# First stage of a hybrid decoder layer: statistics by group of three blocks, loads and bias tables in a new order

## The chip, the cores and the metric

The kernel runs on one core of a Trainium2 chip. A core has five engines with queues of their own: TensorE (PE in the profile, its weight loads PEld), VectorE (DVE), ScalarE (ACT), GpSimd (POOL) and SyncE (SP), which here issues nearly all transfers. The metric is the device time of one execution in microseconds (us), as the median of several; lower is better.

## The reference

One decoder layer over 16 learned meta rows and 1024 tokens, width 1024, all in float32:

```python
h = concatenate([meta, x])
a = rmsnorm(h, ln_mix_pre)                 # h * rsqrt(mean(h*h) + eps) * gain
dq, dk, dv, hq, hf, hi, hg = split(a @ w_in)
y_diff = diff_attention(dq, dk, dv, ...)   # 4 heads, two softmaxes each, T5 bias table by distance
y_hgrn = hgrn2(hq, hf, hi, hg, ...)        # 4 heads of a gated recurrence
h = h + rmsnorm(concatenate([y_diff, y_hgrn]) @ w_out, ln_mix_post)
h = h + rmsnorm(conv_ffn(rmsnorm(h, ln_ffn_pre)), ln_ffn_post)
out = h[16:]
```

The change touches the first lines only: the RMS norm ahead of the input projection, the projections dq, dk and dv of head 0, and the small tables that attention and recurrence need (the relative-position bias, the lower bounds of the gate, the lambda of the differential attention).

## The kernel before

**Precision by halves.** A float32 product is made from three matmuls: each operand is a rounded part (hi) and the remainder (lo), and hi·hi, hi·lo and lo·hi are summed in PSUM. So each operand costs a cast (mostly on ScalarE) and a subtraction (on VectorE or GpSimd): `ahi` and `alo` are the halves of the activations, `wh_` and `wl_` those of the weights from the raw load `wr_` (for dv: `w` from `wv`).

**Blocks and groups.** The rows are nine blocks: block 0 is the 16 meta rows, blocks 1 to 8 are 128 tokens each. Three blocks make a group: 272 columns in group 0, 384 in groups 1 and 2. A projection of one head is 128 output columns; for one group it takes 8 slices of the inner dimension by 3 products, 24 matmuls, each with the weights stationary.

**The first stage**, everything that the change touches, works on a transposed copy of the input (`xt`, tiles `xr`), which can go into the matmuls at once, and on the plain rows (`x`, `xm` for the meta rows), of which only the sums of squares are wanted:
- `x_stat(i)`: for one block ScalarE squares and sums its rows (an activation and the reading of its accumulator), takes the reciprocal root by a logarithm and an exponential, and scales an identity matrix by it (tile `dg`).
- `x_spread(g)` (L297): TensorE multiplies ones with the three `dg` of a group, which spreads the factors over all partitions in a PSUM tile `prs`.
- `x_norm`, `x_hi`, `x_lo`: for each of 8 slices VectorE multiplies `xr` by gain and factor, ScalarE casts to `ahi`, VectorE or GpSimd subtracts to `alo`.
- `Kinds.mm` (L843) issues a projection's matmuls (tiles `pi_dq`, `pi_dk`, `pi_dv`), and `out()` evacuates a finished one: q and k by ScalarE and VectorE in halves (`q`, `k`, `kl`), v by ScalarE into `vt`, which `flush()` later has TensorE transpose (`pn_va`) and ScalarE copy to `avn`.
- `smalls` and `lam_terms` compute the gate's bounds (`lg`, `lmx`, `lb` and others) and lambda (`lv`, `le`, `nlam`) from small loads. `bias_tables` loads a one-hot matrix (`ohr`) and the table (`tb`), casts both (`oh`, `tbb`), and for each head multiplies them (L354, tile `pb`), copies the product to `rb`, subtracts a column, fills a third of it and stores it to `rsc` in DRAM, from where attention reads it.

After the stage the heads follow: `proj_step` (L248, L250, L252) issues the matmuls of all later projections, hf, hq, hi and hg of head 0 first, with attention woven between, and `load_split` (L165) loads their weights.

**What sets the order.** TensorE's instructions run as the program issues them, everywhere. For VectorE, ScalarE and GpSimd a planner sets the order by its own costs, but while `state["ordered"]` is true (the first stage up to the marked line) each instruction issued through `V`, `A` or `G` keeps its place in program order on its engine. SP's transfers, issued through `SY`, are left to the planner throughout. A tile waits for the buffer of its tag: the tag `m` has five PSUM banks in this stage (`prs`, `pn`, `pb` and the projections of group 1 use it), the tag `ip` three; `rb` has one buffer, `ss` and `dg` three, and the plain rows of blocks 1 to 8 go through four slots. The weight halves `wh` and `wl` have four buffers, which dq and dk of head 0 fill and hf and hq take next.

## Time and profile before

| | us |
|---|---|
| median of 3 runs (1293.88 to 1297.57) | 1294.78 |
| profiled execution | 1295.81 |
| its span | 1293.8 |
| TensorE busy in the span (97%) | 1256.9 |
| VectorE (70%), ScalarE (53%), GpSimd (40%) | 910.2, 692.1, 511.8 |

The span runs from the first to the last instruction of the profiled execution; the 2.0 us between span and time lie around it. Busy time is the sum of an engine's instructions; TensorE's matmuls overlap one another, so a busy TensorE need not be at its peak, and the granted clock (1.00 is full) is shown beside it. In the rows below, `out<-in` names the tiles by the program's names, `xN` is a count of merged instructions, and the bracket at the end gives the idle time of the engine ahead of the row and what ended it. A timeline row begins with its start and its length in us; L58 is the helper through which the engines other than TensorE are issued, so those rows are told apart by their tiles.

### The profile page before, as it was taken

How to read it: one execution, taken by the hardware profiler on the slowest of the kernel's cores; microseconds unless marked ns; L12 is line 12 of the kernel's file. 1: busy time of each engine (PE TensorE's matmuls, PEld its weight loads, DVE VectorE, ACT ScalarE, POOL GpSimd, SP SyncE). 2: the span in 40 equal slices, each digit the busy share in tenths (PEclk: the TensorE clock that was granted, in tenths of full speed). 3: DMA queues.
4: the chain of work that ended last, by engine and by line, in shares of the span. 5: the costliest groups of instructions: out<-in, count | busy, mean ns of one | idle time of the engine just before them, and what ended most of it. 6: DMA issues, size and time to landing. Idle time of an engine off the chain costs nothing.

```text
span 1293.8 us, 25973 instructions
## 1 busy us (share of the span) xinstructions
PE 1256.9 (97%) x10108; PEld 1174.3 (91%) x10108; DVE 910.2 (70%) x1496; ACT 692.1 (53%) x1653; POOL 511.8 (40%) x394
## 2 busy tenths in 40 slices
PE   5699999999999999999999999999999999999997
PEld 5599999999999999778899999999999998878886
DVE  3557455654656465558798888888888967797586
ACT  6665457545754665346775445445444454554454
POOL 5232233342314220345056776776776731010121
PEclk9899999999999999999999999999999999999999
DMA  8236356545565531778512222222223237965363
GB/s 323 80 101 114 91 107 131 107 89 112 118 129 88 114 91 52 231 242 283 200 31 93 90 66 91 90 66 91 82 67 99 66 107 248 353 196 171 90 212 122
DMA packets 117710, 169.28 MB, mean 131 GB/s; under 512 B 10370, under 2 KB 58050, under 8 KB 117588
## 3 DMA queue, kind: packets, MB, share of 16 engines
q1 hardware_dynamic: 94356, 156.10, 37.2%
q0 software_dynamic: 23232, 11.54, 7.6%
q8 instruction: 79, 1.29, 0.4%
q14 instruction: 43, 0.35, 0.1%
HBM read 138.50 MB, written 52.17 MB: 147 GB/s over the span
## 4 chain that ended last, share of the span: by engine, by line
PE 45%; DVE 5%; ACT 2%; issue 1%; DMA 0%; SPq 0%; DVEq 0%; ACTq 0%
PE pd L1562 5%; PE pd L1563 4%; PE pd L1561 4%; PE pb L1388 4%; PE pb L1387 4%; PE pb L1389 4%; PE pc L1388 3%; PE pc L1387 3%; PE pc L1389 3%; PE pa L1388 3%; PE pa L1387 3%; PE pa L1389 3%; DVE xh L58 1%; DVE t L58 1%; ACT a L58 1%
## 5 line engine op out<-in xcount | busy, mean ns | idle before, releaser
L1388 PE MATMUL pb<-t,uh 128*128 128x258 f32 x504 | 141.0, 280 | 0.8 <-DVE t L58 0.8
L1387 PE MATMUL pb<-t,uh 128*128 128x258 f32 x504 | 140.5, 279 | 0.8 <-DVE u L58 0.8
L1389 PE MATMUL pb<-t,ul 128*128 128x258 f32 x504 | 140.2, 278 | 0.0
L1562 PE MATMUL pd<-wl,gh 128*128 128x512 f32 (+1 forms) x312 | 121.0, 388 | 1.5 <-DVE wl L58 1.5
L1561 PE MATMUL pd<-wh,gh 128*128 128x512 f32 (+1 forms) x312 | 120.7, 387 | 0.5 <-DVE x L58 0.5
L1563 PE MATMUL pd<-wh,gl 128*128 128x512 f32 (+1 forms) x312 | 120.8, 387 | 0.0
L58 DVE SCALAR_TENSOR_TENSOR c<-uu,cwt,c 128x514 f32<-128x514 f32 (+1 forms) x88 | 107.0, 1215 | 0.0
L58 DVE SCALAR_TENSOR_TENSOR c<-ug,cwt,c 128x514 f32<-128x514 f32 (+1 forms) x88 | 101.6, 1155 | 0.0
L1388 PEld LDWEIGHTS pb<-t,uh 128*128 128x128 f32 x504 | 94.8, 188 | 1.0 <-DVE t L58 1.0
L1387 PEld LDWEIGHTS pb<-t,uh 128*128 128x128 f32 x504 | 94.8, 188 | 1.0 <-DVE u L58 1.0
L58 ACT ACTIVATE c<-c 128x514 f32<-128x514 f32 (+1 forms) x44 | 27.9, 634 | 125.5 <-DVE c L58 125.5
L1389 PEld LDWEIGHTS pb<-t,ul 128*128 128x128 f32 x504 | 94.8, 188 | 0.0
L1388 PE MATMUL pc<-t,uh 128*128 128x258 f32 (+1 forms) x336 | 94.3, 281 | 0.0
L1387 PE MATMUL pc<-t,uh 128*128 128x258 f32 (+1 forms) x336 | 94.2, 280 | 0.0
L1388 PE MATMUL pa<-t,uh 128*128 128x258 f32 (+1 forms) x336 | 94.0, 280 | 0.0
L1389 PE MATMUL pc<-t,ul 128*128 128x258 f32 (+1 forms) x336 | 93.9, 279 | 0.0
L1387 PE MATMUL pa<-t,uh 128*128 128x258 f32 (+1 forms) x336 | 93.7, 279 | 0.0
L1389 PE MATMUL pa<-t,ul 128*128 128x258 f32 (+1 forms) x336 | 93.5, 278 | 0.0
L58 POOL TENSOR_TENSOR ul<-ws,uh 128x512 fp32r<-128x512 f32 x42 | 69.2, 1647 | 59.7 <-ACT uh L58 59.7
L58 POOL TENSOR_TENSOR ws<-ra,ra 128x512 f32<-128x512 f32 x42 | 67.4, 1604 | 61.5 <-DVE c L58 31.3
L58 POOL TENSOR_TENSOR c<-c,c 128x514 f32<-128x514 f32 (+1 forms) x44 | 69.0, 1567 | 54.9 <-ACT c L58 49.9
L58 DVE TENSOR_TENSOR ul<-ra,uh 128x512 fp32r<-128x512 f32 x43 | 41.2, 959 | 46.9 <-POOL ul L58 46.9
(384 smaller groups left out, 4187.5 us busy)
## 6 DMA issues: line engine op xcount, KB each, us to landing
ra<-in_wup_dram SPq DMA_DIRECT2D x88, 256.0 KB, 2.6
mp<-msc SPq DMA_DIRECT2D x23, 512.0 KB, 5.6
tsc<-in_wdown_dram SPq DMA_DIRECT2D x44, 256.0 KB, 5.1
wi<-tsc SPq DMA_DIRECT2D x44, 256.0 KB, 3.1
gi<-gsc SPq DMA_DIRECT2D x33, 256.0 KB, 4.6
wi<-in_wdown_dram SPq DMA_DIRECT2D x33, 256.0 KB, 5.3
gsc<-c SPq DMA_DIRECT2D x22, 257.0 KB, 2.1
tsc<-in_wdown_dram POOLq DMA_DIRECT2D x22, 256.0 KB, 7.1
```

The costliest lines, as they stand in the source:

```text
L58: ins = call(*args, **kw)
L1387: T.matmul(pt, hi[:, s], th[:, k], start=(first and k == 0), stop=False, skip_group_check=True)
L1388: T.matmul(pt, hi[:, s], tl[:, k], start=False, stop=False, skip_group_check=True)
L1389: T.matmul(pt, lo[:, s], th[:, k], start=False, stop=(k == 3), skip_group_check=True)
L1561: T.matmul(py, gh[:, s], wh, start=(k == 0 and pr not in (3, 7)), stop=False, skip_group_check=True)
L1562: T.matmul(py, gh[:, s], wl, start=False, stop=False, skip_group_check=True)
L1563: T.matmul(py, gl[:, s], wh, start=False, stop=(k == NH - 1), skip_group_check=True)
```

## The change

Statistics are taken for a whole group: the three sums of squares go into the columns of one tile, with one logarithm and one exponential for the three, and the diagonals are made on VectorE. The meta rows are squared and summed on VectorE, the other blocks on ScalarE. Block 5 gets its own place beside the meta rows, in the buffer that later holds the transposed rows of group 2. The loads are issued in a new order, with the one-hot matrix and the bias table ahead of the second transposed group; the casts of both come ahead of the statistics of group 1. Hi and lo products of the first half of dq and dk are issued together. The statistics of group 2 come ahead of the evacuation of group 0; the tables of heads 0 and 1, then the spread and the norm of group 2, come before the last products of group 1; `alo` of group 2 is made on GpSimd in place of VectorE; dv and dk of group 2 are issued in the ordered part, and the tables of heads 2 and 3 between the products of dq and dk. `smalls` and `lam_terms` come after all this in the program, and `issue_after` puts them behind the last norm on VectorE and the last cast on ScalarE.

```diff
-    def x_stat(i):
-        r = rows(i)
-        ss = zp.tile([P, 1], F32, tag="ss", name=f"ss{i}", bufs=3)
-        A.activation(x_rows[i][:r], x_rows[i][:r], AF.Square, accum_out=ss[:r])
-        rstd_of(ss[:r], ss[:r], D)
-        dg = zp.tile([P, P], F32, tag="dg", name=f"dg{i}", bufs=3)
-        A.mul(dg[:r, :r], ident[:r, :r], ss[:r])
-        return dg
+    def x_stats(g, on_vector=()):
+        blks = range(*GROUPS[g])
+        ss = zp.tile([P, 3], F32, tag="ss", name=f"ss{g}", bufs=3)
+        if g == 0:
+            V.memset(ss, 1.0)
+        for c, i in sorted(enumerate(blks), key=lambda b: b[1] == 0):
+            r = rows(i)
+            if i in on_vector:
+                V.tensor_tensor(x_rows[i][:r], x_rows[i][:r], x_rows[i][:r], op=ALU.mult)
+                V.reduce_sum(ss[:r, c:c + 1], x_rows[i][:r], axis=AX.X)
+            else:
+                A.activation(x_rows[i][:r], x_rows[i][:r], AF.Square, accum_out=ss[:r, c:c + 1])
+        rstd_of(ss, ss, D)
+        res = {}
+        for c, i in enumerate(blks):
+            r = rows(i)
+            res[i] = zp.tile([P, P], F32, tag="dg", name=f"dg{i}", bufs=3)
+            V.tensor_scalar(res[i][:r, :r], ident[:r, :r], ss[:r, c:c + 1], None, ALU.mult)
+        return res
...
-    def bias_tables():
+    def bias_loads():
...
+        return oh, raw, tb
+
+    def bias_casts(oh, raw, tb):
         tbb = zp.tile([64, HEADS, P], F32R, tag="tbb", name="tbb", bufs=1)
         A.copy(oh, raw)
...
+        return tbb, oh
-        for h in range(HEADS):
...
+    def bias_table(h, tbb, oh):
+        pt = ps_m(f"pb{h}")
+        T.matmul(pt[:, :384], tbb[:, h], oh, start=True, stop=True)
+        rb = zp.tile([P, 512], F32, tag=f"wv{h}", name=f"rb{h}", bufs=1)[:, :384] if h < 2 else zp.tile([P, 384], F32, tag="rb", name=f"rb{h}", bufs=1)
+        V.tensor_copy(rb, pt[:, :384])
+        V.tensor_scalar(rb[:, :256], rb[:, :256], rb[:, 0:1], None, ALU.subtract)
+        V.memset(rb[:, 256:], NEG)
+        SY.dma_start(rsc[h].rearrange("(p c) -> p c", p=P), rb)
...
-    x_rows = {0: zp.tile([P, KD * 3 * P], F32, tag="xr2", name="xm", bufs=1)[:, :D]}
-    for i in range(1, NBLK):
-        x_rows[i] = slots[(i - 1) % 4]
+    spare = zp.tile([P, KD * 3 * P], F32, tag="xr2", name="xm", bufs=1)
+    x_rows = {0: spare[:, :D], 5: spare[:, D:2 * D]}
+    for n, i in enumerate((1, 2, 3, 4, 6, 7, 8)):
+        x_rows[i] = slots[n % 4]
...
     for i in (1, 2, 0):
         load_x(i)
-    SY.dma_start(gcol, gpre)
     open_xt(0)
     open_xt(1)
-    for c in range(2):
-        load_xt(0, 4 * c, 4 * c + 4)
-        for j in range(2):
-            load_raw(j, c)
-    for i in (3, 4):
+    load_raw(0, 0)
+    load_xt(0, 0, 4)
+    SY.dma_start(gcol, gpre)
+    load_raw(1, 0)
+    load_xt(0, 4, 8)
+    for j, c in ((0, 1), (1, 1), (2, 0), (2, 1)):
+        load_raw(j, c)
+    for i in (3, 4, 5):
         load_x(i)
-    for c in range(2):
-        load_raw(2, c)
+    bias = bias_loads()
     for c in range(2):
         load_xt(1, 4 * c, 4 * c + 4)
...
-    stats = {i: x_stat(i) for i in (1, 2, 0)}
+    stats = x_stats(0, (0,))
     spread = {0: x_spread(0, stats)}
-    for i in (5, 6):
+    for i in (6, 7):
         load_x(i)
-    open_xt(2)
-    for c in range(2):
-        load_xt(2, 4 * c, 4 * c + 4)
     w_hi(0, 0, G)
+    w_lo(0, 0, G)
     w_hi(1, 0, G)
-    w_lo(0, 0, G)
     w_lo(1, 0, G)
     for k in range(KD):
         x_norm(0, k, spread[0])
         x_hi(0, k)
+        if k == 3:
+            w_hi(0, 1, A)
         if k == 5:
-            for j in range(2):
-                w_hi(j, 1, A)
+            w_hi(1, 1, A)
...
-    for i in (3, 4, 5):
-        stats[i] = x_stat(i)
-    for i in (7, 8):
-        load_x(i)
+    for m in range(2):
+        G.memset(az[m], 0.0)
+    tbb = bias_casts(*bias)
+    stats = x_stats(1)
+    open_xt(2)
+    for c in range(2):
+        load_xt(2, 4 * c, 4 * c + 4)
+    load_x(8)
     dq, dk, dv = first = [Kinds(j, 0, ps_in) for j in range(3)]
-    for half in range(2):
-        for k in range(4 * half, 4 * half + 4):
-            for kd in (dq, dk):
-                kd.mm(k, 0, ahi)
-    for half in range(2):
+    for k in range(4):
         for kd in (dq, dk):
-            kd.part(half, 1, ahi)
+            kd.mm(k, 0, ahi)
+            kd.mm(k, 1, ahi)
+    for k in range(4, KD):
+        for kd in (dq, dk):
+            kd.mm(k, 0, ahi)
+    for kd in (dq, dk):
+        kd.part(1, 1, ahi)
...
+    stats = x_stats(2)
     for kd in first:
         kd.out()
-    for m in range(2):
-        G.memset(az[m], 0.0)
-    for i in (6, 7, 8):
-        stats[i] = x_stat(i)
     second = [Kinds(j, 1, ps_m) for j in range(3)]
     for k in range(KD):
         for kd in second:
             kd.mm(k, 0, ahi)
             kd.mm(k, 1, ahi)
+    for h in range(2):
+        bias_table(h, *tbb)
+    spread[2] = x_spread(2, stats)
+    for k in range(KD):
+        last_norm = x_norm(2, k, spread[2])
+        last_hi = x_hi(2, k)
+        x_lo(2, k, G)
     flush()
-    smalls()
-    lam_terms()
-    tables = bias_tables()
-    next(tables)
-    for j, kd in enumerate(second):
+    for kd in second:
         for half in range(2):
             kd.part(half, 0, alo)
-        if j == 0:
-            spread[2] = x_spread(2, stats)
+        kd.out()
+    dq, dk, dv = [Kinds(j, 2, ps_in) for j in range(3)]
     for k in range(KD):
-        x_norm(2, k, spread[2])
-        x_hi(2, k)
-    for kd in second:
+        for kd in (dq, dk):
+            kd.mm(k, 0, ahi)
+            kd.mm(k, 1, ahi)
+    for h in range(2, HEADS):
+        bias_table(h, *tbb)
+    flush()
+    for kd in (dq, dk):
+        for half in range(2):
+            kd.part(half, 0, alo)
         kd.out()
-    for k in range(KD):
-        last_lo = x_lo(2, k, V)
-    dq = Kinds(0, 2, ps_in)
     for w, a in ((0, ahi), (1, ahi), (0, alo)):
         for half in range(2):
-            dq.part(half, w, a)
-    dq.out()
-    flush()
+            dv.part(half, w, a)
+    dv.out()
     state["ordered"] = False
-
-    def head0():
-        for j, (m, name, evac) in enumerate(tiles):
-            if j:
-                yield from proj_group(2, parts[j], name, evac)
-
-    interleave(head0(), [tables], 2600)
+    with tc.issue_after(last_norm.ins), tc.issue_after(last_hi.ins):
+        smalls()
+        lam_terms()
```

More of the change, by code (lines that the diff above doesn't have):

```diff
@@ L301, in x_norm @@
     def x_norm(g, k, pt):
-        V.scalar_tensor_tensor(xr[g][:, k], xr[g][:, k], gcol[:, k:k + 1], pt, ALU.mult, ALU.mult)
+        return V.scalar_tensor_tensor(xr[g][:, k], xr[g][:, k], gcol[:, k:k + 1], pt, ALU.mult, ALU.mult)
     def x_hi(g, k):
-        A.copy(ahi[:, k, cols(g)], xr[g][:, k])
+        return A.copy(ahi[:, k, cols(g)], xr[g][:, k])
     def x_lo(g, k, eng):
@@ L351, in bias_tables @@
         V.tensor_tensor(tbb[32:], tbr[32:].to_broadcast([32, HEADS, P]), tbb[32:].bitcast(F32), op=ALU.subtract)
-        for h in range(HEADS):
-            pt = ps_m(f"pb{h}")
-            T.matmul(pt[:, :384], tbb[:, h], oh, start=True, stop=True)
-            rb = zp.tile([P, 384], F32, tag="rb", name=f"rb{h}", bufs=1)
-            V.tensor_copy(rb, pt[:, :384])
-            V.tensor_scalar(rb[:, :256], rb[:, :256], rb[:, 0:1], None, ALU.subtract)
-            G.memset(rb[:, 256:], NEG)
-            SY.dma_start(rsc[h].rearrange("(p c) -> p c", p=P), rb)
-            yield
+        return tbb, oh
[7 more added lines that the diff above has]
+        SY.dma_start(rsc[h].rearrange("(p c) -> p c", p=P), rb)
     def to_nat(dst, srcT, b0, b1, name):
```

## The prediction

> **What bounds the kernel now.** I read the busy time of two stretches first (columns: stretch, length, then busy time and instructions of PE, PEld, DVE, ACT and POOL, granted clock, DMA share, GB/s), then PE's own waits in the first 80 us, longest first.
>
> ```profile
> 0.00:75.00 75.00, 51.93 (x248) 45.89 (x249) 32.21 (x75) 45.00 (x105) 28.16 (x38) 0.91 0.54 192
> 75.00:1293.80 1218.80, 1205.01 (x9862) 1128.37 (x9861) 877.95 (x1421) 647.10 (x1549) 483.66 (x356) 1.00 0.45 127
> ```
>
> ```profile
> PE prs L297 <- ACT dg L58: 10.6, 1, 10.6
> PE pb L354 <- DVE tbb L58: 7.6, 1, 7.6
> ...
> PE pi_dq L843 <- DVE alo L58: 1.9, 1, 1.9
> ```
>
> TensorE stands idle for 23.1 of the first 75 us (75.00 - 51.93) and for 13.8 of the other 1218.8. From 75 us on only the amount of matmul work counts, and the change leaves that alone; what it can win or lose lies before the first matmul of the HGRN projections (hf). The timeline says where that is, and what stands ahead of the 7.6 us wait:
>
> ```profile
> 37.53 0.27 PE L368 MATMUL pn_va<-ident,vt 128*128 128x128 f32 x1
> ...
> 42.16 0.16 DVE L58 TENSOR_TENSOR lmx<-lg 128x4 f32<-128x4 f32 x1 [5.11 <-ACT lg L58]
> ...
> 44.77 0.68 DVE L58 TENSOR_TENSOR tbb<-tb,tbb 32x512 fp32r<-32x512 f32 x1
> ...
> 74.58 0.29 PE L248 MATMUL pi_hf<-ahi,wh_hf 128*128 128x272 f32 x1
> ```
>
> The table matmul pb needs only tbb, but VectorE, in program order, reaches tbb after the small terms, and these stood 5.11 us for lg, an activation queued on ScalarE behind the squares of group 2. Idling also costs clock (the column before DMA's share):
>
> ```profile
> 46.00:48.00 2.00, 2.00 (x7) 1.82 (x7) 0.93 (x2) 0.00 (x0) 0.20 (x1) 0.50 0.00 0
> ...
> 56.00:58.00 2.00, 0.68 (x4) 0.36 (x3) 1.94 (x4) 1.93 (x5) 0.00 (x0) 1.00 0.00 0
> 58.00:60.00 2.00, 1.32 (x3) 0.66 (x3) 1.99 (x5) 0.13 (x1) 0.00 (x0) 0.88 0.00 0
> 60.00:62.00 2.00, 2.00 (x6) 1.25 (x5) 1.85 (x4) 0.62 (x1) 0.50 (x1) 0.50 0.00 0
> ...
> 66.00:68.00 2.00, 2.00 (x12) 1.85 (x10) 0.15 (x1) 0.62 (x1) 0.14 (x1) 0.91 0.37 125
> ```
>
> After the 7.6 us wait the matmuls run at half clock, and again from 60 to past 66, after the 1.9 us wait for alo.
>
> **Part 1: up to the first spread.**
>
> ```profile
> DMA to landing us min/median/max: 4.5/4.5/4.5
> ```
>
> ```profile
> 1.64 0.43 SPq L281 DMA_DIRECT2D xm<-in_meta_dram  x1
> ...
> 8.38 1.04 ACT L58 ACTIVATE xm<-xm 16x1024 f32<-16x1024 f32 x1
> ...
> 10.55 1.73 PE L297 MATMUL prs<-dg,ones 16*128 16x16 f32 x6 [10.55 <-ACT dg L58]
> ...
> 12.32 3.36 DVE L58 SCALAR_TENSOR_TENSOR xr<-xr,gcol,prs 128x272 f32<-128x272 f32 x8 [12.32 <-PE prs L297]
> ...
> 13.41 0.57 PE L843 MATMUL pi_dq<-ahi,wh_dq 128*128 128x272 f32 x1 [1.13 <-ACT ahi L58]
> 15.59 2.90 DVE L58 TENSOR_TENSOR alo<-xr,ahi 128x272 fp32r<-128x272 f32 x8
> 15.91 3.72 POOL L58 TENSOR_TENSOR wl_dq<-wr_dq,wh_dq 128x512 fp32r<-128x512 f32 x1 [2.77 <-ACT wh_dq L58]
> 18.16 1.11 PE L843 MATMUL pi_dq<-ahi,wl_dq 128*128 128x272 f32 x4
> 19.60 1.27 POOL L58 TENSOR_TENSOR wl_dk<-wr_dk,wh_dk 128x512 fp32r<-128x512 f32 x1
> 22.00 1.16 PE L843 MATMUL pi_dv<-ahi,w 128*128 128x272 f32 x8
> ```
>
> Before, ScalarE does squares, logarithm, exponential and diagonal for one block after another and ends with the meta block. Now the two big squares come first and the meta rows go to VectorE: a multiply and a sum, 1024 columns each. A 272-column subtraction on VectorE goes at 0.36 us (2.90 for eight), 1.3 ns a column with its overhead, so each of the two costs 1.1 to 1.36; I take 1.2. The meta rows land at 6.1 (1.64 + 4.5), the sum is there at 8.5, logarithm and exponential take it to 9.1, the first of three short diagonals to 9.6. The first spread thus starts at **9.6 in place of 10.55**. Bounds: 8.5, were VectorE free of cost, and 10.5, were each of its two passes at 1.7. ScalarE, at 1.04 and an accumulator read from 7.2 on, would have had the meta square at 8.4 too: the move to VectorE is worth nothing by itself; the gain is the two small chains that fall away.
>
> From the spread to the first projection matmul 2.86 us pass (13.41 - 10.55), so that starts at 12.5. Its order now takes hi and lo of the first weight half together: 16 matmuls, then 8 of the second half, at 0.226 us each while the clock is cold (18.16, four in 0.9): 5.4 us, to 17.9. Next come the lo parts of the second half, which GpSimd makes. VectorE's alo subtractions hold GpSimd up: 3.72 us for a piece that takes 1.27 alone. They now run at about 14.8 to 17.7, so wl_dq is ready at 18.5, wl_dk at 19.8, the two of dv at 22.3. TensorE waits 0.6 and 0.4 us, and starts the remaining 40 matmuls, less a few, at 20.7. The clock was warm at 22.00, with 0.127 a matmul (eight in 1.16 less the tail of the last); if that stays, six go cold and 34 warm: group 0 ends at 20.7 + 1.3 + 4.3 = **26.3**, and at 25.0 if the clock warms by 18, since the work is denser now. I take T1 = 25.9 for the second spread, bounds 25.0 and 27.5.
>
> Is the second spread's input there? On ScalarE the cast of the one-hot table now stands ahead of the squares of group 1, and waits for a load:
>
> ```profile
> 0.00:10.00 10.00, 0.00 (x0) 0.00 (x0) 0.00 (x0) 6.73 (x15) 3.65 (x14) 1.00 0.80 262
> 10.00:20.00 10.00, 8.00 (x31) 7.17 (x32) 6.17 (x16) 7.43 (x20) 7.16 (x5) 1.00 1.03 412
> ```
>
> In SP's new order the loads up to the table come to 5.5 MB (x 0 to 5: 2.7, first transposed group 1.1, six weight pieces 1.6). 2.62 MB have moved by 10 us, and the rest at 412 GB/s takes 7 us: it leaves at 17 and lands at about 19. Casts on ScalarE end before (17.4), so it stands still until 19.2, casts 0.5, squares three blocks at 1.25 (1.04 and the accumulator) to 23.4, and the diagonals are done on VectorE at 24.6. That is 1.3 us ahead of T1: hidden, with that as its cover. Each us that the table lands after 20.5 moves T1 by a us.
>
> **Part 2: groups 1 and 2**, counted from the start of the second spread (26.98 before, T1 = 25.9 now).
>
> ```profile
> 26.98 0.83 PE L297 MATMUL prs<-dg,ones 128*128 128x128 f32 x6
> 27.85 4.29 DVE L58 SCALAR_TENSOR_TENSOR xr<-xr,gcol,prs 128x384 f32<-128x384 f32 x8 [9.36 <-PE prs L297]
> ...
> 28.50 4.19 ACT L58 CAST ahi<-xr 128x384 fp32r<-128x384 f32 x8 [4.34 <-DMA lg<-in_lbl_dram]
> 29.06 0.44 PE L843 MATMUL pi_dq<-ahi,wh_dq 128*128 128x384 f32 x1 [1.25 <-ACT ahi L58]
> ...
> 29.08 7.87 POOL L58 TENSOR_TENSOR alo<-xr,ahi 128x384 fp32r<-128x384 f32 x8 [5.73 <-ACT ahi L58]
> ...
> 32.59 0.79 ACT L58 ACTIVATE q<-pi_dq 64x272 fp32r<-64x272 f32 x2
> ```
>
> ```profile
> 34.32 0.89 DVE L58 TENSOR_TENSOR kl<-pi_dk,k 64x272 fp32r<-64x272 f32 x2
> ...
> 46.28 0.56 DVE L58 COPY rb<-pb 128x384 f32<-128x384 f32 x1 [0.84 <-PE pb L354]
> 46.88 0.37 DVE L58 TENSOR_SCALAR rb<-rb 128x256 f32<-128x256 f32 x1
> ```
>
> Unchanged: TensorE's 48 hi and lo matmuls end at +10.55 (37.53 - 26.98; 0.176 each), ScalarE's casts at +5.7, GpSimd's alo at +10.0. New from there on:
> - ScalarE squares group 2 ahead of the evacuations: three at 1.25 from +5.7, logarithm, exponential: +10.1. VectorE, which stands for it, has the diagonals at +10.7. The evacuations of group 0, queued behind on both, run from +10.1; from ScalarE's first to VectorE's last they took 2.62 us (32.59 to 35.21): +12.75.
> - TensorE does two table matmuls at once, +11.5, as tbb has been there since 20 us: the 7.6 us wait is **gone**. What is late next is the third spread. PSUM has five banks of its kind, three hold group 1, so it needs the first table's bank, and VectorE copies that (0.56) only behind the evacuations: +13.3. So TensorE waits 1.9 us, and the spread ends at +14.2. Bounds: none of it, if a bank is free, and 3 if the copy slips behind one more evacuation.
> - VectorE finishes the two tables (copy, 0.37, a fill that I take at 0.2 as on GpSimd, twice) at +15.0; their stores pass on SP behind loads that have landed. It normalises to +19.3, ScalarE casts to +19.9; GpSimd subtracts from +16.2 at 0.98 each: alo of group 2 is there at +24.1, and no longer after the evacuations on VectorE, which were behind the 1.9 us wait and the cold stretch after it.
> - TensorE meanwhile turns v of group 0 (0.8) and runs 24 alo matmuls of group 1 (4.2): +19.5; then dq and dk of group 2, 32 by 0.176: +25.1; two tables and v of group 1: +26.9; 16 alo matmuls, whose input came at +24.1: +29.7; 24 of dv: +33.9. A us for the changes between these pieces: **+34.9**. Before it was 74.58 - 26.98 = 47.6.
>
> On SP, x5 is loaded early into the buffer of the meta rows, which later takes the last transposed group. Table and x5 push the second transposed group back by 0.6 MB, 1.5 us, to about 23, ahead of T1. The last group's load now waits for x5's square (23.4), and x8 and the small terms' loads behind it; 2.1 MB at 412 GB/s bring x8 by 30.5, and its square starts at T1 + 8.2 = 34.1: hidden by 3.6 us, beyond which the third spread moves a us for a us.
>
> The small terms, now queued after the last normalisation and the last cast, lie beside these matmuls; their first user is the evacuation of hf, 12 us later. The az fills and bias casts lie on queues that wait anyway.
>
> **The sum.** hf starts at 25.9 + 34.9 = 60.8 in place of 74.58: 13.8 us less, 1.1 from part 1 and 12.7 from part 2. The profiled execution took 1295.81 (span 1293.80 and 2.0 around it), 1.0 above the median: 1282.0 for it, and **1281.0** against the median of 1294.78.
>
> **Rivals.**
> - The clock falls in the 1.9 us wait for the third spread. For it: the wait for alo, as long, is followed by half clock from 60 to past 66; against: the stretch 56:58 was emptier (0.68 us of work) than this one. Five us at half clock lose 2.5: **1283.5**. The Trainium skill, "TensorE: Matmul & The Clock Gate", section "HAM oscillation — how this bites in real kernels", gives the rule "no PE-idle gaps >~3.4µs". By that rule this wait would cost no clock and the time would stay at 1281; the trace does not bear it out, as 1.9 us of wait with thin work around it were followed by 0.50.
> - The gain is given back at the seam to hf:
>
> ```profile
> 60.80 0.62 ACT L58 CAST wh_hf<-wr_hf 128x512 fp32r<-128x512 f32 x1 [2.67 <-issue]
> ...
> 61.50 1.49 POOL L58 TENSOR_TENSOR wl_hf<-wr_hf,wh_hf 128x512 fp32r<-128x512 f32 x1 [14.39 <-ACT wh_hf L58]
> ```
>
>   hf's halves take the buffers of dq's, free at +28 and +29; cast and subtraction take 2.1 us, so they fit ahead of +34.9. But the evacuations of dq, dk and dv are now all in program order. If the casts are queued behind dv's, TensorE stands 2.1 us and two more cold: **1285**.
> - The change doesn't do what it says: SP isn't held to program order, and the table's loads may go out as late as before, when they were issued at 28.06 and landed at 31. They then hold ScalarE ahead of the squares, T1 moves to 37 (31 + 0.5 + 3.7 + diagonals and a wait), and hf starts at 72: **1292**, no change that can be told. Against: their buffers are free from the start.
>
> ```profile
> 28.06 0.33 SPq L345 DMA_DIRECT2D ohr<-in_onehot_dram  x1
> ```
>
> - Slower: the 28 weight tiles of the heads are cast in an order that the planner makes from its own times, which all shift. If an evacuation that waits for TensorE comes to stand ahead of the cast in each, TensorE waits for cast and subtraction (2.1 us). It decides where the idle 13.8 us after the stage grow past 31.5 (by the 13.8 won and 3.9): nine tiles do that; at twelve tiles the loss is 25 us: **1306**. For it: these orders aren't written out; against: today there is hardly any such wait.
>
> **How the numbers follow.** A measurement tells 0.3% (3.9 us) from no change. Forecast 0.55, clock 0.18, seam 0.11, table late 0.10, slower 0.06. Table late gives 0.03 faster (landing earlier than at 31) and 0.07 same; so faster 0.55 + 0.18 + 0.11 + 0.03 = 0.87, same 0.07, slower 0.06. For the range, no wait for the bank, the warm T1 and no price at the changes give 4 us less (1277); bounds 27.5 of T1, 3 us of bank wait and the seam together give 1288. Below 1276.5 and above 1289 I leave 2 in 10.
>
> **What would show it.** The first spread at 9.6 and the second at 25 to 27.5; no wait for tbb; a wait of about 2 us of the third spread for the copy of the first table; no half clock after 50 us; hf's first matmul near 61; idle time after it as before. I'm wrong if ScalarE waits for the one-hot load beyond 20.5, if hf waits for its weights, or if the later idle time grows.

## The result, and the profile after

The changed kernel takes 1280.64 us (median of four, 1279.91 to 1283.92) against 1294.54 for the kernel before on the same chip: a ratio of 0.9893, with a 95% interval of 0.987 to 0.9916. It is faster, by 13.9 us; the forecast was 1281.0. The profiled execution took 1279.91, with a span of 1278.1. Of all executions reported below one, of the kernel with the spread ahead of the tables, took 2070.18 us at a mean granted clock of 0.559 and is left out of that kernel's median.

The same two stretches as before (stretch, length, busy time and instructions of PE, PEld, DVE, ACT and POOL, granted clock, DMA share, GB/s):

```profile
0.00:75.00 75.00, 60.74 (x354) 58.38 (x355) 48.33 (x112) 48.32 (x120) 36.55 (x46) 0.98 0.62 208
75.00:1278.00 1203.00, 1189.50 (x9757) 1112.97 (x9755) 867.63 (x1392) 636.18 (x1513) 481.74 (x352) 1.00 0.45 128
```

After 75 us TensorE idles for 13.5 us, where it idled for 13.8 before. The stretch ahead of that lost 8.8 us of idle time (23.1 to 14.3), and its clock rose from 0.91 to 0.98: half clock lasted 13.7 us of it before and 3.4 after. PE's waits in the first 70 us, longest first:

```profile
PE prs L308 <- DVE dg L58: 10.1, 1, 10.1
PE pi_dq L860 <- ACT ahi L58: 2.4, 2, 1.2
PE prs L308 <- DVE rb L58: 1.6, 1, 1.6
```

The waits for `tbb` (7.6) and for `alo` (1.9) are gone; the new one is the third spread's wait for the copy of the first table (`rb`). The timeline (start, length, engine, line, operation, tiles, count, idle time before it and what ended it):

```profile
6.66 1.21 DVE L58 TENSOR_TENSOR xm<-xm 16x1024 f32<-16x1024 f32 x1 [5.80 <-DMA xm<-in_meta_dram]
7.91 1.21 DVE L58 TENSOR_REDUCE ss<-xm 16x1 f32<-16x1024 f32 x1
9.23 0.30 ACT L58 ACTIVATE ss<-ss,eps 128x3 f32<-128x3 f32 x1 [1.98 <-DVE ss L58]
10.14 1.76 PE L308 MATMUL prs<-dg,ones 16*128 16x16 f32 x6 [10.14 <-DVE dg L58]
13.03 0.57 PE L860 MATMUL pi_dq<-ahi,wh_dq 128*128 128x272 f32 x1 [1.13 <-ACT ahi L58]
14.71 1.28 POOL L58 TENSOR_TENSOR wl_dq<-wr_dq,wh_dq 128x512 fp32r<-128x512 f32 x1 [2.51 <-ACT wh_dq L58]
15.21 6.81 DVE L58 TENSOR_TENSOR alo<-xr,ahi 128x272 fp32r<-128x272 f32 x8
...
19.68 0.51 ACT L58 CAST oh<-ohr 64x384 fp32r<-64x384 f32 x1 [2.21 <-DMA ohr<-in_onehot_dram]
23.93 0.68 DVE L58 TENSOR_SCALAR dg<-ident,ss 128x128 f32<-128x128 f32 x3 [0.85 <-ACT ss L58]
25.30 0.83 PE L308 MATMUL prs<-dg,ones 128*128 128x128 f32 x6
...
35.94 0.62 PE L370 MATMUL pb<-oh,tbb 64*128 64x384 f32 x2
38.21 0.94 PE L308 MATMUL prs<-dg,ones 128*128 128x128 f32 x6 [1.64 <-DVE rb L58]
39.24 0.30 PE L383 MATMUL pn_va<-ident,vt 128*128 128x128 f32 x1
...
39.51 2.88 PE L860 MATMUL pi_dq<-alo,wh_dq 128*128 128x384 f32 x8
40.65 7.84 POOL L58 TENSOR_TENSOR alo<-xr,ahi 128x384 fp32r<-128x384 f32 x8 [5.38 <-ACT ahi L58]
...
51.02 0.61 PE L370 MATMUL pb<-oh,tbb 64*128 64x384 f32 x2
...
51.86 1.63 PE L860 MATMUL pi_dq<-alo,wh_dq 128*128 128x384 f32 x8
52.84 0.62 ACT L58 CAST wh_hf<-wr_hf 128x512 fp32r<-128x512 f32 x1 [0.22 <-PE pi_dq L860]
58.95 0.29 PE L248 MATMUL pi_hf<-ahi,wh_hf 128*128 128x272 f32 x1
```

hf starts at 58.95 in place of 74.58, 15.6 us earlier, and the span is 15.7 shorter: the whole gain was made before hf, and none of it was given back. Two rows show the one blemish: eight `alo` matmuls take 2.88 us at 39.5 and 1.63 us at 51.9. The clock (the column before DMA's share) was halved in between:

```profile
36.00:38.00 2.00, 0.57 (x3) 0.24 (x2) 1.93 (x5) 1.32 (x4) 0.00 (x0) 1.00 0.10 35
38.00:40.00 2.00, 1.70 (x11) 1.54 (x12) 1.93 (x8) 0.00 (x0) 0.00 (x0) 0.89 0.22 78
40.00:42.00 2.00, 2.00 (x8) 2.00 (x7) 2.00 (x5) 1.90 (x4) 1.35 (x2) 0.50 0.84 236
42.00:44.00 2.00, 2.00 (x11) 2.00 (x10) 2.00 (x6) 1.96 (x5) 2.00 (x3) 0.76 0.82 149
```

So the forecast's time came true, and in this execution the mechanism of its clock rival as well. The experiments ask which parts of the change made the gain, what the 1.64 us wait costs, and whether the rest of the forecast's steps hold.

### The profile page after: what moved, and what is told of

Its sections match the earlier page's. It is cut to its first block, busy times and chain, and to the rows that moved or that the text cites. A ratio compares the mean times of both kernels' runs of the same rounds, so it can differ in the third digit from the quotient of the medians.

```text
span 1278.1 us, 25957 instructions
## 1 busy us (share of the span) xinstructions
PE 1250.2 (98%) x10108; PEld 1171.4 (92%) x10108; DVE 916.0 (72%) x1504; ACT 684.5 (54%) x1630; POOL 518.3 (41%) x398
## 4 chain that ended last, share of the span: by engine, by line
PE 46%; DVE 4%; ACT 2%; DMA 2%; issue 1%; POOL 1%; SPq 0%; DVEq 0%; POOLq 0%
PE pd L1581 5%; PE pd L1582 4%; PE pb L1407 4%; PE pb L1406 4%; PE pd L1580 4%; PE pb L1408 4%; PE pc L1407 3%; PE pc L1406 3%; PE pc L1408 3%; PE pa L1407 3%; PE pa L1406 3%; PE pa L1408 3%; DMA gi<-gsc 1%; DVE xh L58 1%; DVE t L58 1%
```

## The experiments

Each kernel was compared with the kernel before on its own chip. The start of hf is also counted from the second spread, which leaves out what comes before it. All times are in us. The kernels of one set were measured side by side on one chip.

| kernel | set | first spread | second spread | hf starts | hf after second spread | median (n) | ratio (95%) |
|---|---|---|---|---|---|---|---|
| before | | 10.55 | 26.98 | 74.58 | 47.60 | 1294.54 (4) | 1 |
| after | | 10.14 | 25.30 | 58.95 | 33.65 | 1280.64 (4) | 0.9893 (0.987 to 0.9916) |
| meta squares on ScalarE | 1 | 9.27 | 24.44 | 58.06 | 33.62 | 1277.8 (1) | |
| wait filled by own work | 1 | 10.19 | 25.37 | 56.61 | 31.24 | 1276.33 (4) | 0.9847 (0.9833 to 0.9862) |
| spread ahead of the tables | 1 | 9.85 | 25.04 | 55.67 | 30.63 | 1280.36 (3) | 0.9876 (0.986 to 0.9893) |
| bias part alone | 1 | 10.80 | 27.12 | 67.19 | 40.07 | 1287.87 (4) | 0.994 (0.9924 to 0.9957) |
| bias part undone | 2 | 9.58 | 24.77 | 63.45 | 38.68 | 1282.76 (4) | 0.9896 (0.9881 to 0.991) |
| bias loads late | 2 | 10.06 | 30.57 | 65.16 | 34.59 | 1286.84 (1) | |
| alo on VectorE, in the loop | 2 | 9.72 | 24.88 | 64.47 | 39.59 | 1285.08 (4) | 0.9913 (0.9899 to 0.9928) |
| wait filled by extra work | 2 | 9.86 | 25.04 | 57.09 | 32.05 | 1277.41 (4) | 0.9852 (0.9836 to 0.9869) |
| after, second profile | 3 | 10.00 | 25.19 | 57.24 | 32.05 | 1278.93 (4) | 0.9868 (0.9854 to 0.9883) |
| ScalarE and filled wait | 3 | 9.18 | 24.36 | 55.59 | 31.23 | 1276.94 (4) | 0.9849 (0.9834 to 0.9863) |
| ScalarE and spread first | 3 | 9.75 | 24.93 | 55.96 | 31.03 | 1277.05 (4) | 0.9855 (0.9837 to 0.9874) |
| alo on VectorE, behind | 3 | 9.98 | 25.18 | 57.23 | 32.05 | 1278.19 (4) | 0.986 (0.9844 to 0.9876) |

### Meta squares back on ScalarE

```diff
-    stats = x_stats(0, (0,))
+    stats = x_stats(0)
```

> The changed kernel with one edit undone: the meta rows are squared on ScalarE, behind blocks 1 and 2, no longer on VectorE. Theory (the move to VectorE is worth nothing): in the changed kernel VectorE had the meta sum at 9.1 us and the first spread began at 10.14; ScalarE, free at 7.26, would have it at 8.5, so the first spread starts at 9.4 to 10.2 here. Rival (the move is what brings the spread forward): ScalarE takes 1.25 us more for it and the spread starts at 11 or later. The second spread is set by TensorE and starts at 24.6 to 25.4 by the theory, 26 or later by the rival.

```profile
7.12 1.04 ACT L58 ACTIVATE xm<-xm 16x1024 f32<-16x1024 f32 x1
8.35 0.30 ACT L58 ACTIVATE ss<-ss,eps 128x3 f32<-128x3 f32 x1
9.27 1.75 PE L308 MATMUL prs<-dg,ones 16*128 16x16 f32 x6 [9.27 <-DVE dg L58]
```

In this timeline the logarithm starts at 8.35, against 9.23 with the squares on VectorE. One profile could be chance, so all of them count: the first spread starts at 9.93 on average in the nine profiles with the squares on VectorE (9.58 to 10.19), at 9.40 in the three with them on ScalarE (9.18 to 9.75). So moving the meta squares costs about half a us, on averages whose ranges just overlap; both starts of this kernel, 9.27 and 24.44, lie a little ahead of what the theory expected. The gain of part 1 then lies in the rest of it, the single chain of logarithm and exponential, with diagonals on VectorE and the loads in a new order; no run takes these apart.

### The wait filled, by own work and by extra work

The first kernel, whose edit is shown, moves eight `alo` products of group 1 between the tables and the third spread. The second adds eight matmuls there instead, whose result then counts alo·hi of dq, group 1, twice.

```diff
     for h in range(2):
         bias_table(h, *tbb)
+    for half in range(2):
+        second[0].part(half, 0, alo)
     spread[2] = x_spread(2, stats)
...
-            kd.part(half, 0, alo)
+            if kd is not second[0]:
+                kd.part(half, 0, alo)
```

> The changed kernel, with the eight alo matmuls of dq of group 1 issued between the second table and the third spread, where TensorE waited 1.64 us for VectorE and the clock then stood at half from 39 to 43.5. Nothing else moves; VectorE's order is the same, so the third spread still starts near 38.2. Theory (that wait is what cools the clock, and costs 1.6 us and some 2 us of half clock): no half clock between 36 and 46, hf starts at 55 to 56 in place of 58.95, time 3 to 4 us under the changed kernel. Rival 1 (the clock falls anyway, since the stretch is thin): only the 1.6 us come, or less, and the half clock stays. Rival 2 (VectorE's norm of group 2 bounds what follows): TensorE waits later for ahi or alo of group 2, and hf starts as before, at 58 to 59.

```profile
36.56 1.66 PE L860 MATMUL pi_dq<-alo,wh_dq 128*128 128x384 f32 x8
38.27 0.94 PE L308 MATMUL prs<-dg,ones 128*128 128x128 f32 x6
```

> The changed kernel with eight more matmuls of 384 columns in the 1.64 us wait ahead of the third spread. They add alo times the hi weights to dq of group 1 a second time, so that dq counts this product twice; no work is saved. Theory (the wait itself costs nothing beyond its length, but the clock that falls behind it costs about 2 us): the clock stays at 1.00 from 36 to 46, hf starts at 56.5 to 57.5 in place of 58.95 and the time is 1.5 to 2.5 us under the changed kernel, with more work done. Rival (the half clock lies beside VectorE's norm and costs nothing): the clock stays up, but hf starts at 58.5 to 59.5 and the time is the same as that of the changed kernel.

```profile
36.22 1.66 PE L938 MATMUL pi_dq<-alo,wh_dq 128*128 128x384 f32 x8
37.93 0.94 PE L308 MATMUL prs<-dg,ones 128*128 128x128 f32 x6
```

In both timelines the third spread follows at +12.9 after the second, as in the kernel after, but with no idle time ahead of it, and neither is cold between 36 and 46 us. The extra work, which shortens nothing by itself, has hf at +32.05, 1.60 before the profile of the kernel after shown above; the moved work has it at +31.24, and at 56.61 in place of the 55 to 56 expected. It saves 0.81 more and not the 1.4 that eight matmuls take at 0.175 us from one start to the next, because a later piece now comes early: TensorE waits 0.5 us for `q` on VectorE at the transposes of v.

### The kernel after once more

Neither of these two shows by itself that the wait cools the clock: for that the same program has to be seen again.

> The changed kernel once more, beside the other three: 1279.5 to 1282, hf near 58.95.

Timeline of the second profile:

```profile
38.08 0.94 PE L308 MATMUL prs<-dg,ones 128*128 128x128 f32 x6 [1.64 <-DVE rb L58]
...
57.24 0.29 PE L248 MATMUL pi_hf<-ahi,wh_hf 128*128 128x272 f32 x1
```

The same wait of 1.64 us, with the same pieces of work around it, costs no clock at all here. hf comes at +32.05, and both it and the median of 1278.93 are lower than expected. So the wait can cool the clock and need not. Of five profiles with this wait three were cold behind it (after, squares on ScalarE, alo in the loop) and two were not (this one, and alo behind). The price of the cold stretch is 33.65 - 32.05 = 1.6 us; the second profile has the same +32.05 as the kernel with extra work, so what that work won was the clock and nothing else.

The traces also show what sets the cold profiles apart. The clock changes only on the edges of a grid with steps of 3.41 us, as the last section works out. These are the stretches of the grid around the wait, in the first profile (wait from 36.57 to 38.21), in the second (36.44 to 38.08), and with alo behind (36.44 to 38.07):

```profile
36.14:39.56 3.42, 1.68 (x12) 1.20 (x11) 3.28 (x11) 1.18 (x4) 0.00 (x0) 1.00 0.05 17
```

```profile
34.51:37.92 3.41, 1.93 (x10) 1.36 (x9) 3.21 (x8) 2.63 (x8) 0.64 (x1) 1.00 0.35 130
37.92:41.34 3.42, 3.17 (x20) 3.01 (x21) 3.35 (x10) 1.39 (x3) 0.81 (x1) 1.00 0.45 122
```

```profile
36.89:40.31 3.42, 2.15 (x14) 1.99 (x15) 3.31 (x10) 0.74 (x2) 0.00 (x0) 1.00 0.22 66
```

In the first profile the whole wait lies in one stretch, which is left with 1.68 us of matmul work, and the next stretch is cold. In the two others an edge cuts the wait, and each stretch keeps more.

### The bias part, alone and undone

First the kernel before, with only loads, casts and the first table early and the small terms late:

```diff
+    bias = bias_loads()
     for c in range(2):
         load_xt(1, 4 * c, 4 * c + 4)
...
+    tbb = bias_casts(*bias)
     for i in (3, 4, 5):
         stats[i] = x_stat(i)
...
-    smalls()
-    lam_terms()
-    tables = bias_tables()
-    next(tables)
+    bias_table(0, *tbb)
...
+    with tc.issue_after(last_norm.ins), tc.issue_after(last_hi.ins):
+        smalls()
+        lam_terms()
...
```

> The kernel before, with one part of the change alone: one-hot matrix and table are loaded ahead of the second transposed group and cast ahead of the statistics of group 1, and small terms and lambda come behind the last norm of group 2; the statistics stay by block, alo of group 2 on VectorE behind the evacuations. Theory (the 7.6 us wait is the order on VectorE, but the evacuations ahead of the squares and alo on VectorE keep their share): the table matmul starts near 38.5, the third spread at 41 to 42 in place of 48.9 (ScalarE's squares end at 41.6), hf at 64 to 67 in place of 74.6; time 1284 to 1288. Rival (nearly all of the change lies in this part): hf at 60 to 62, time 1280 to 1282.

```profile
41.80 0.49 PE L297 MATMUL prs<-dg,ones 128*128 128x128 f32 x2 [1.25 <-ACT dg L58]
...
50.97 3.97 PE L848 MATMUL pi_dq<-alo,wh_dq 128*128 128x384 f32 x8 [1.92 <-DVE alo L58]
```

```profile
50.35 3.84 DVE L58 TENSOR_TENSOR alo<-xr,ahi 128x384 fp32r<-128x384 f32 x8
```

The 7.6 us wait is gone and hf comes 7.4 us earlier, about half of the change's gain, at 67.19, a little past the 64 to 67 expected. Of the other 8.2, 1.8 lie ahead of the second spread (27.12 against 25.30). For the rest these rows show two waits that the change removes: the third spread still waits for the diagonals made one by one on ScalarE, and the `alo` matmuls for VectorE, where `alo` stands behind the evacuations. Eight of them then take 3.97 us, as they follow VectorE's eight subtractions one by one, and the clock is at half from 52.4 to 59.3.

Then the reverse, the kernel after with small terms and casts back in their old place ahead of the first table:

```diff
-    tbb = bias_casts(*bias)
...
+    smalls()
+    lam_terms()
+    tbb = bias_casts(*bias)
     for h in range(2):
         bias_table(h, *tbb)
...
-    with tc.issue_after(last_norm.ins), tc.issue_after(last_hi.ins):
-        smalls()
-        lam_terms()
```

> The changed kernel with one part undone: small terms, lambda and the casts of one-hot matrix and table stand again, in program order, ahead of the first table (behind the squares of group 2 and the evacuations of group 0); the loads stay early. Theory (the order on VectorE makes the wait): VectorE reaches tbb only behind some 4 us of small operations, TensorE waits 4 to 6 us at the table from 36 us on and runs cold after it, hf starts at 63 to 66 in place of 58.95, time 4 to 7 us above the changed kernel (1285 to 1288). Rival (the early squares had already taken the wait away, so the place of the small terms no longer matters): hf at 59 to 61, time within 2 us of the changed kernel.

```profile
41.24 0.97 PE L370 MATMUL pb<-oh,tbb 64*128 64x384 f32 x2 [5.77 <-DVE tbb L58]
42.62 1.65 PE L308 MATMUL prs<-dg,ones 128*128 128x128 f32 x6 [0.40 <-DVE rb L58]
```

The wait returns, at 5.8 us, with half clock from 40 to 47 us. hf moves to +38.68, 5.0 later than in the first profile of the kernel after and 6.6 later than in the second, which was warm; at 63.45 it is inside the expected 63 to 66, and so is the wait. The time, 1282.76, is 2.2 us under the low end of the expectation; the section on the reasons comes back to that.

### The bias loads late

```diff
-    bias = bias_loads()
...
     for i in (6, 7):
         load_x(i)
+    bias = bias_loads()
```

> The changed kernel, with the loads of one-hot matrix and table issued behind those of x6 and x7, 2.6 MB later. Theory (the cast of the one-hot matrix holds ScalarE ahead of the squares of group 1, a us for a us): the one-hot lands 6 us later, near 25.5 in place of 19.6, the second spread moves from 25.3 to 30 to 32, and hf to 63 to 66. Rival (there is slack, or the planner moves the cast's place): the second spread starts below 27.

```profile
26.00 0.51 ACT L58 CAST oh<-ohr 64x384 fp32r<-64x384 f32 x1 [8.60 <-DMA ohr<-in_onehot_dram]
...
30.57 1.65 PE L308 MATMUL prs<-dg,ones 128*128 128x128 f32 x6 [5.16 <-DVE dg L58]
```

The cast of the one-hot matrix is on ScalarE ahead of the squares of group 1, so a load that lands at 26 in place of 19.7 puts the second spread at 30.57 and hf at 65.16. 6.3 us later on the queue became 5.3 us on the path. The cover that the forecast gave this load is real, and thin: the kernel after has its diagonals at 24.61 (23.93 + 0.68) for a spread at 25.30.

### alo of group 2 on VectorE

```diff
         last_hi = x_hi(2, k)
-        x_lo(2, k, G)
+        x_lo(2, k, V)
```

> The changed kernel with alo of group 2 on VectorE in place of GpSimd, at the same place of the program. Theory (what counts is that alo stands ahead of the evacuations of group 1, not which engine makes it): VectorE subtracts from 43.7 to 47.7, well ahead of its first use near 52; the evacuations move back 4 us and have that much slack; hf starts at 58.5 to 60, time within 2 us of the changed kernel. Rival (the four us on VectorE come back at the seam, as the evacuations and the tables behind them hold banks): hf starts at 61 to 63, time 2 to 4 us above it.

```profile
40.27 0.56 DVE L58 TENSOR_TENSOR alo<-xr,ahi 128x384 fp32r<-128x384 f32 x1 [0.58 <-ACT ahi L58]
40.75 0.61 DVE L58 SCALAR_TENSOR_TENSOR xr<-xr,gcol,prs 128x384 f32<-128x384 f32 x1
41.94 0.56 DVE L58 TENSOR_TENSOR alo<-xr,ahi 128x384 fp32r<-128x384 f32 x1 [0.58 <-ACT ahi L58]
```

hf comes at 64.47, not at the 58.5 to 60 that the theory gave: 5.9 us further from the second spread than in the first profile of the kernel after, which was cold as this one is, and 7.5 further than in the second. These rows show why: each slice goes from VectorE (norm) to ScalarE (cast) and back (alo), and VectorE in order stands for the cast each time, 1.67 us a slice where norm and alo together take 1.0. The next kernel asks whether it was the engine or the order, with the same eight subtractions on VectorE behind the eight norms:

```diff
         last_hi = x_hi(2, k)
-        x_lo(2, k, G)
+    for k in range(KD):
+        x_lo(2, k, V)
```

> The changed kernel with alo of group 2 on VectorE, behind all eight norm slices. Inside the loop VectorE had taken 1.66 us a slice, each subtraction waiting for its cast on ScalarE. Theory (that chain, and not VectorE's 4 us, made the loss of 5 us): VectorE subtracts from 43.7 to 47.7, the evacuations of group 1 end at 54, hf starts at 59 to 60.5, time within 2 us of the changed kernel. Rival (the 4 us on VectorE themselves come back, as evacuations and tables behind them hold banks): hf at 61.5 or later, time 3 us or more above it.

```profile
39.39 4.16 DVE L58 SCALAR_TENSOR_TENSOR xr<-xr,gcol,prs 128x384 f32<-128x384 f32 x8
43.48 3.83 DVE L58 TENSOR_TENSOR alo<-xr,ahi 128x384 fp32r<-128x384 f32 x8
```

hf is at +32.05, as in the second profile of the kernel after. It was the order. The move of `alo` to GpSimd is thus worth nothing against a well-placed VectorE; what it saved was the place behind the evacuations.

### The spread ahead of the tables

Another way around the 1.64 us wait: the third spread comes straight after the products of group 1, and the tables of all four heads behind the products of group 2.

```diff
-    for h in range(2):
-        bias_table(h, *tbb)
     spread[2] = x_spread(2, stats)
...
-    for h in range(2, HEADS):
+    for h in range(HEADS):
         bias_table(h, *tbb)
```

> The changed kernel, with the third spread right behind the hi and lo products of group 1 and all four tables behind the products of group 2. The spread takes a free bank and needs only the diagonals (35.8), so it starts at 36.0 in place of 38.2, and VectorE normalises from 37.6 (behind the evacuations of group 0) in place of 39.5. Theory (the wait for the first table's copy is a matter of banks and of VectorE's order): no wait at the third spread, no half clock, hf starts at 54.5 to 56, time 3 to 4.5 us under the changed kernel. Rival (four tables in a row bring a new wait, as the last two share one buffer and TensorE needs a bank for each): TensorE waits 2 to 4 us at the tables near 47 and hf starts at 57 to 59.

```profile
55.96 0.56 DVE L58 COPY rb<-pb 128x384 f32<-128x384 f32 x1 [2.42 <-PE pi_dv L860]
...
58.96 1.12 DVE L58 TENSOR_TENSOR kl<-pi_dk,k 64x384 fp32r<-64x384 f32 x2
```

```profile
60.23 0.52 PE L385 MATMUL pn_va<-ident,vt 128*128 128x128 f32 x3 [2.11 <-DVE kl L58]
```

The spread comes at 35.59 and hf at 55.67, the earliest but one, as the theory said. Then 2.1 us are given back behind hf: the last table shares its buffer with the one before it, so its copy stands 2.42 us on VectorE (the row names pi_dv; in the kernel after the same copy waits 2.00 for the store `rsc<-rb`), and the evacuations of dq and dk stand behind it, up to 60.08. TensorE's transposes need the bank that these hold, and the median, 1280.36, is no better than that of the kernel after. The theory did not have this wait; the rival named the shared buffer, but put the wait at the tables near 47 and hf at 57 to 59.

### Two together

```diff
-    stats = x_stats(0, (0,))
+    stats = x_stats(0)
...
+    for half in range(2):
+        second[0].part(half, 0, alo)
     spread[2] = x_spread(2, stats)
...
-            kd.part(half, 0, alo)
+            if kd is not second[0]:
+                kd.part(half, 0, alo)
```

> The changed kernel with two edits: the meta rows squared on ScalarE, and dq's alo matmuls of group 1 ahead of the third spread. If the two gains (0.9 us and 2.3 us at hf's start) have separate causes they add: hf at 55.4 to 56.2, time 4 to 5 us under the changed kernel. If the second only lies beside VectorE's norm, as TensorE gets ahead of it, hf stays at 56.3 to 56.8.

hf starts at 55.59, inside the expected range: the two gains add. The time is 1276.94, 2.0 under the kernel after of the same set where 4 to 5 were expected. Up to 1.6 of what is missing may be the cold stretch, which the kernel after did not have in that set's profile; its other three executions have no profile, so this is not shown. All its four times (1274.71 to 1277.2) lie under all four of the kernel after (1277.67 to 1280.47). The last kernel has the squares on ScalarE, the spread first and two tables amid the products of group 2:

```diff
...
     for k in range(KD):
+        if k == 4:
+            for h in range(2):
+                bias_table(h, *tbb)
         for kd in (dq, dk):
```

> The changed kernel with the meta rows squared on ScalarE, the third spread right behind the hi and lo products of group 1, and the first two tables halfway through the products of group 2, the other two where they are. Theory (the earlier kernel with four tables in a row lost 2.1 us at the seam because the last table waits for the buffer's store and holds the evacuations behind it on VectorE): with two tables early the last table's copy is back near 52, no wait at the seam, hf at 54 to 55.2, time 5 to 6 us under the changed kernel. Rival (the tables amid the products take a bank that isn't free, or VectorE is late for the evacuations): TensorE waits 1 to 3 us between 42 and 50, time 2 to 4 us under it.

```profile
PE pn_va L383 <- ACT vt L58: 0.7, 1, 0.7
```

That is PE's only wait from 36 to 62 us, so the 2.1 us at the seam are gone with the tables apart. But the first spread came at 9.75 and hf at 55.96, later than the 54 to 55.2 expected; the median, 1277.05, is 1.9 under the kernel after of the same set, where 5 to 6 were expected, and no better than that of the kernels with the filled wait.

## Why the prediction was right, and where it was off

The median came within 0.4 us. Some of that is luck: the profiled executions went from 1295.81 to 1279.91, 15.9 us less, where the forecast had 13.8; the medians are 13.9 apart since the profiled execution of before lay 1.3 above its median, and that of after 0.7 below. Errors of opposite sign also cancelled in part: the terms for change-overs were 2.85 too large, and a cold stretch of 1.6 was not counted. Step by step:

- **First spread, 9.6: it was 10.14.** The two VectorE passes took 1.21 each as priced (1.2). The meta rows landed at 6.66, not 6.1, which is all of the miss. "The move to VectorE is worth nothing by itself" was right in that it gains nothing; it costs half a us.
- **Second spread, 25.9: it was 25.30.** From first spread to second 15.16 us passed where the forecast had 16.3. The step that failed is "VectorE's alo subtractions hold GpSimd up": it came the other way round. GpSimd's four pieces ran from 14.71 to 20.31 (1.28 for the first, 3.72 before) and VectorE's eight subtractions took 6.81 in place of 2.90. TensorE did not wait for GpSimd, so the 0.6 and 0.4 us that the forecast had it wait fell away; for VectorE it waited 0.17 us twice, ahead of the last two `alo` slices of dq. The rest is the clock: matmuls are 0.125 us apart from 19.1 us on, where they were still 0.226 apart at 20 us before. That is near the forecast's case of an early warm clock (25.0), and 25.9 was a choice between its two cases.
- **The one-hot load, 19.2, and the diagonals, 24.6: they were 19.68 and 24.61**, hidden as forecast. The late loads show what it costs without that cover.
- **The tables and the third spread, +13.3 with a wait of 1.9: it was +12.91 with 1.64**, for the copy into `rb` that was named. That the 7.6 us wait goes is shown from both sides: the bias part alone wins 7.4 us, its undoing loses 5.0 to 6.6.
- **From the second spread to hf, +34.9: it was +33.65**, in spite of a cold stretch that the forecast did not count. Without it the second profile has +32.05. The difference of 2.85 lies in the terms for change-overs and one slip: the third spread 0.4 early, 0.3 too much in the forecast's own sum (14.2, 0.8 and 4.2 make 19.2, not 19.5), v of group 0 at 0.27 in place of 0.8 (39.24 to 39.51), tables and v of group 1 at 0.84 in place of 1.8 (51.02 to 51.86), and "a us for the changes between these pieces", of which the profile shows none. The matmuls were priced right: 24 of `alo` from 39.38 to 43.66 in the second profile, 4.28 for 4.2.
- **The clock rival** (1283.5, 2.5 us) took place in the profiled execution, at 1.6 us. Half clock lasted 3.4 us there, not five. It was hidden in the time since the terms above were too large by more. Its argument, that a short wait with thin work around it can cool the clock, holds, though not every time; what it lacked is the grid on which the clock changes.
- **The seam, the late table, the slower case** did not come. `wh_hf` is cast at 52.84, six us ahead of its use; the idle time after 75 us is 13.5. The kernel with the spread first shows that a seam of that kind is there: 2.1 us, of another cause (the last table's buffer).

What stays open is how times follow hf. Span less the start of hf should be the same for kernels that differ only before it. It is 1219.2 for before and after, but runs from 1216.6 (bias part undone) to 1222.2 (squares on ScalarE and spread first), and the same program had 1219.15 and 1221.5 in its two profiles. In the second of these part of it shows as a wait far behind the stage, with a dip of the clock behind it (PE's waits from 61 us on, then the stretch 480 to 540 in the first and in the second profile):

```profile
PE pl L490 <- issue: 2.1, 1, 2.1
```

```profile
480.00:540.00 60.00, 59.20 (x735) 49.27 (x734) 30.55 (x58) 25.58 (x63) 17.01 (x16) 1.00 0.50 162
```

```profile
480.00:540.00 60.00, 57.48 (x707) 46.73 (x706) 27.82 (x53) 23.60 (x53) 16.09 (x16) 0.97 0.49 157
```

So a shift of hf by less than some 3 us can't be read from the total time of a few executions. This fits the kernels whose hf came as expected and whose time did not (bias part undone, both combinations); that it is their cause was not shown for each.

## What to carry to other kernels

Find what stands ahead of a waiting matmul's input in program order on its engine: here a table's cast stood behind small terms of the gate that were ready at 42.9 and first read at 80.5, and having the loads and casts early and these terms late was worth half the gain. When work is moved to another engine, ask whether the engine or the place in the queue was the matter: `alo` on VectorE costs 5.9 to 7.5 us inside the loop, where each slice stands for ScalarE, and nothing behind it. And a gap on TensorE, once found, is best closed with matmuls that have to run anyway; the three profiles with the gap filled stayed warm, of the five with it only two.

## What the hardware showed that was not expected

**A wait of 1.64 us halves the clock in some executions and not in others, and where it falls on a grid of equal steps tells which.** Cold in three of five profiles, at 1.6 us in the two where the rest was equal (+33.65 and +33.62 against +32.05). Half clock lasts 3.41 us in all three (39.56 to 42.97 in the first), twice 6.83 in the kernel before (42.46 to 49.29 and 59.53 to 66.36), and 10.24 with the bias loads late (29.42 to 39.66): one, two and three steps. From the change at 42.97 to the last one of that profile, at 1275.18, there are 361 steps of 3.4133 us. Counted back by that step from a later change of the same profile (522.62 in the second, 1272.51 with alo behind), the edges of the two warm profiles are known too. The wait lies whole in one stretch of the grid in the three cold profiles, which leaves 1.68, 1.67 and 1.77 us of matmul work in it; an edge cuts it in the two warm ones, whose stretches keep at least 1.93 and 2.15. So here the limit lies near half a stretch. In all fourteen profiles no stretch with more than 1.77 us of matmul work is followed by half clock, though a few with a little less stay warm (1.61 from 544.46 to 547.87 with extra work). The grid lies differently in each execution, and no run moves it on purpose.

The Trainium skill, "TensorE: Matmul & The Clock Gate", section "What's actually happening", says that activity is judged in free-running windows of 3.4 us, so that the point of change depends on where in a window the work falls. The trace agrees, with steps of 3.41 us and two outcomes of the same wait in the same program. The Trainium skill, "TensorE: Matmul & The Clock Gate", section "HAM oscillation — how this bites in real kernels", gives "no PE-idle gaps >~3.4µs" as the rule. As a safe bound it does not hold here, where a gap of 1.64 us was enough.

**Between VectorE and GpSimd the one that starts first comes off better, and not only for one instruction.** Before, VectorE's subtractions began at 15.59 and GpSimd's at 15.91: VectorE took 2.90 for eight, and GpSimd 3.72 for one, which ended only behind all eight. After, GpSimd began at 14.71 and VectorE at 15.21: GpSimd took 1.28 for the first piece and 1.48 to 1.49 for the next three. VectorE took 6.81 for its eight: 1.08 to 1.52 each for the four that ran beside GpSimd's pieces, 0.43 each for the last four, as all eight had taken before. The kernels with the order of the kernel after repeat the 6.81 to within 0.05 us (6.81 to 6.85 in eleven more profiles), and the bias part alone, in the order of before, has 2.90 and 3.73. The Trainium skill, "SBUF — State Buffer", section "Who interferes with whom", says that the order of issue decides who blocks. The trace agrees: a shift of 0.8 us between the two starts (0.32 one way, 0.50 the other) went with a loss of 2.4 us on GpSimd or of 3.9 on VectorE. No run changed the starts and nothing else.
